# Attention weights, keys and queries turned by VectorE in 32x32 blocks through DRAM instead of by TensorE

## The chip, the cores and the metric

The kernel runs on one core of a Trainium2 chip. The metric is the device time of one execution in microseconds (us). Before the change the median of three runs is 1805.57 us (1801.99 to 1807.5). The engines are named as in the profile: PE is TensorE (PEld its loading of weights), DVE is VectorE, ACT is ScalarE, POOL is GpSimd, SP is SyncE. SP and ACT each have a queue through which they issue DMAs. A difference of less than 0.3% (5.4 us) can't be told from none with runs like these.

## The reference

A backbone of two layers over 256 latent tokens and 256 context tokens of width 2048, in fp32. The even layer has 16 attention heads of width 128 and a state-space mixer side by side, the odd layer a gated short convolution. Only the attention part matters here:

```python
q = rms_norm(heads(cols(p, COL_Q, NA_WIDTH, 0), NA_HEADS, NA_HEAD_DIM), q_norm_g)
k = rms_norm(heads(cols(p, COL_K, NA_WIDTH, 0), NA_HEADS, NA_HEAD_DIM), k_norm_g)
...
s_lat = jnp.einsum('bqhd,bkhd->bhqk', qr, kb) * scale + bias      # per row of the token grid
s_lat = jnp.where(mask, s_lat, -jnp.inf)
s_ctx = jnp.einsum('bqhd,bkhd->bhqk', qr, k_ctx) * scale
pr = jax.nn.softmax(jnp.concatenate([s_lat, s_ctx], axis=-1), axis=-1)
ya = pr[..., :n] @ vb + pr[..., n:] @ v_ctx
ya = ya * jax.nn.silu(gate)
```

So a head has 256 queries and 512 keys. Every product is done with about fp32 precision: each operand is split into a high part and a low rest in the type fp32r, and three products are summed (high x high, low x high, high x low).

## The kernel before

**Work on TensorE.** Nearly all of its time goes into the projections: the weight matrices come in blocks of 128x1024 (512 KB) by SP's queue into five `raw` buffers (L379), ACT casts each into `wH` (L409), DVE subtracts to get `wL` (L416), and PE multiplies (L198). There are three `wH` and three `wL` buffers, so ACT and DVE can prepare two blocks ahead of the one that PE uses. A raw buffer is free for the next load when DVE's subtraction is done.

**Attention.** The heads come in four groups of four, `a` = 0 to 3. When the projections of a group are done, `kq_gen` (L927) takes the products of queries (2 tiles of 128 tokens x 4 heads) and keys (4 tiles): squares summed on ACT (L936), the reciprocal root on POOL, the norm on DVE into a `tmp` tile (L945). To multiply queries by keys, head width has to lie on the partitions; so each tile is turned by four TensorE transposes of 128x128 (`turn`, L202) into a PSUM bank, and ACT (keys, L962) or DVE (queries, with the gains of the norm, L964) copies it to `KT` or `QT`. `head_gen` (L998) then does one head: the splits `kH`, `kL`, `qH`, `qL` (L1041 to L1045), the scores for two tiles of 128 queries, maximum and bias on DVE (L1019), the exponent on ACT (L1024), the division by the sum on DVE (L1028, L1029). The weights have to be turned too: per query tile four TensorE transposes into a bank, then `PH` by ACT (L1065) and `PL` by DVE (L1067), and twelve products with the values, whose result goes through DVE (L1087) and `put_mix` to a DRAM tensor `mixd`. After all heads and the state-space groups, `mix_gen` reads `mixd` back, and the output projection runs in three sweeps over 16 pairs of rows, the last two of which in their order are heads 12 to 15. `res_gen` adds the gated result to x, `turn_gen` turns that for the odd layer.

**What sets the order.** Each engine runs its instructions in the order in which the program issues them. That order is made while the program is built: pieces of work are Python generators that stop at each point where an engine would have to wait, and a planner (`Plan`, L42) holds an estimated time for every engine and every part of a tile. A generator goes on when its operands are due by that estimate (`may`, L247); PE's stream is the projection, into which the other work is put as soon as it is due. `force` (L300) runs generators when the projection itself needs something. Queues of generators are `urgent`, `side` (the heads) and `back` (the matrix-vector products for the modulation). A generator holds a share of ten `tmp` and nine `half` tiles; `("grow", t, h)` waits until it can have so many, `("cap", t, h)` gives back.

**DMA in the planner.** `add` (L96) counts 450 ns of the engine for an issue; a transfer by ACT's queue is done 1500 ns after the bytes at 270 bytes per ns, which start not before what SP's queue still has to move.

## Time and profile before

| what | value |
|---|---|
| median of three runs | 1805.57 us |
| the profiled execution's own time | 1800.62 us |
| its span, first to last instruction | 1798.8 us |
| PE busy | 1765.1 us, 98% |
| PEld busy | 1493.6 us, 83% |
| DVE busy | 1302.0 us, 72% |
| ACT busy | 796.7 us, 44% |
| DMA | 376.92 MB, mean 210 GB/s |
| granted clock of TensorE | 0.999 |

The profiled execution lies 4.95 us below the median of the runs and just below the fastest of them. Busy time of PE is the union of its matmuls, which overlap one another; so a share of 98% tells that PE hardly ever stands idle, and what one matmul costs is read from the distance of starts in the timeline.

### The profile page before, as it was taken

How to read it: one execution, taken by the hardware profiler on the slowest of the kernel's cores; microseconds unless marked ns; L12 is line 12 of the kernel's file. 1: busy time of each engine (PE TensorE's matmuls, PEld its weight loads, DVE VectorE, ACT ScalarE, POOL GpSimd, SP SyncE). 2: the span in 40 equal slices, each digit the busy share in tenths (PEclk: the TensorE clock that was granted, in tenths of full speed). 3: DMA queues.
4: the chain of work that ended last, by engine and by line, in shares of the span. 5: the costliest groups of instructions: out<-in, count | busy, mean ns of one | idle time of the engine just before them, and what ended most of it. 6: DMA issues, size and time to landing. Idle time of an engine off the chain costs nothing.

```text
span 1798.8 us, 26647 instructions
## 1 busy us (share of the span) xinstructions
PE 1765.1 (98%) x10057; PEld 1493.6 (83%) x10057; DVE 1302.0 (72%) x2121; ACT 796.7 (44%) x1410; POOL 31.1 (2%) x28
## 2 busy tenths in 40 slices
PE   6999999999999999999999999999999999999998
PEld 4677888888888879888888898888878888888887
DVE  5566777878686877685875787787657777777665
ACT  5322544436252455242454343654445444444442
POOL 0000100001000000000001000000000000000000
PEclk9999999999999999999999999999999999999999
DMA  9987654566656556655574566878857777877564
GB/s 343 343 289 256 194 168 126 156 205 196 201 171 190 156 184 200 191 157 167 171 218 119 163 190 194 233 218 286 282 182 229 242 247 226 263 224 247 188 210 153
DMA packets 249217, 376.92 MB, mean 210 GB/s; under 512 B 32656, under 2 KB 104048, under 8 KB 249088
## 3 DMA queue, kind: packets, MB, share of 16 engines
q1 hardware_dynamic: 239792, 366.64, 65.5%
q10 hardware_dynamic: 9296, 8.57, 1.4%
q8 instruction: 79, 1.29, 0.3%
q14 instruction: 50, 0.41, 0.1%
HBM read 368.70 MB, written 7.77 MB: 209 GB/s over the span
## 4 chain that ended last, share of the span: by engine, by line
PE 91%; DMA 3%; DVE 3%; issue 1%; ACT 1%; SPq 0%; POOL 0%; POOLq 0%; DVEq 0%; ACTq 0%
PE bank L198 89%; PE bank L202 3%; DMA tmp<-dram_csr 2%; DVE wL L416 1%; DMA raw<-in_ada_w 0%; DMA tmp<-dram_mixd 0%; DVE acc L803 0%; DMA tmp<-in_x 0%; DVE hL L752 0%; SPq L566 0%; DVE tmp L1381 0%; DVE tmp L1200 0%; ACT wH L409 0%; DVE half L1396 0%; DVE tmp L748 0%
## 5 line engine op out<-in xcount | busy, mean ns | idle before, releaser
L409 ACT CAST wH<-raw 128x1024 fp32r<-128x1024 f32 (+1 forms) x440 | 459.1, 1044 | 684.7 <-PE bank L198 585.5
L416 DVE TENSOR_TENSOR wL<-raw,wH 128x1024 fp32r<-128x1024 f32 (+1 forms) x440 | 531.9, 1214 | 227.0 <-ACT wH L409 224.3
L198 PE MATMUL bank<-h,wH 128*128 128x512 f32 x1024 | 358.7, 395 | 2.7 <-ACT h L1664 1.5
L198 PE MATMUL bank<-hH,wH 128*128 128x256 f32 (+1 forms) x1040 | 343.2, 330 | 0.9 <-ACT wH L409 0.9
L198 PE MATMUL bank<-hL,wH 128*128 128x256 f32 (+1 forms) x1040 | 337.2, 324 | 0.0
L198 PE MATMUL bank<-hH,wL 128*128 128x256 f32 (+1 forms) x1024 | 331.7, 324 | 1.1 <-DVE wL L416 1.1
L198 PE MATMUL bank<-h,wL 128*128 128x256 f32 x1024 | 287.2, 280 | 0.1
L198 PE MATMUL bank<-wH,hH 128*128 128x512 f32 x640 | 257.4, 403 | 4.8 <-ACT hH L746 2.6
L198 PE MATMUL bank<-wL,hH 128*128 128x512 f32 x640 | 250.1, 391 | 0.3 <-DVE wL L416 0.3
L198 PE MATMUL bank<-wH,hL 128*128 128x512 f32 x640 | 249.8, 391 | 0.1
L803 DVE SCALAR_TENSOR_TENSOR acc<-raw,csil,acc 128x512 f32<-128x512 f32 x256 | 191.8, 749 | 59.8 <-DMA raw<-in_ada_w 45.4
L198 PEld LDWEIGHTS bank<-h,wH 128*128 128x128 f32 x1024 | 192.2, 188 | 48.4 <-issue 2.6
L198 PEld LDWEIGHTS bank<-hH,wH 128*128 128x128 f32 x1040 | 197.9, 190 | 18.7 <-issue 2.0
L198 PEld LDWEIGHTS bank<-hL,wH 128*128 128x128 f32 x1040 | 198.0, 190 | 15.4
L198 PEld LDWEIGHTS bank<-hH,wL 128*128 128x128 f32 x1024 | 194.8, 190 | 17.5 <-DVE wL L416 2.1
L198 PEld LDWEIGHTS bank<-h,wL 128*128 128x128 f32 x1024 | 193.6, 189 | 0.4 <-DVE wL L416 0.4
L198 PE MATMUL bank<-wH,mix 128*128 128x512 f32 x512 | 162.8, 393 | 0.0
L198 PEld LDWEIGHTS bank<-wH,hH 128*128 128x128 f32 x640 | 120.3, 188 | 35.3 <-issue 6.6
L198 PEld LDWEIGHTS bank<-wH,hL 128*128 128x128 f32 x640 | 120.2, 188 | 25.4 <-DVE hL L752 0.6
L198 PEld LDWEIGHTS bank<-wL,hH 128*128 128x128 f32 x640 | 120.3, 188 | 24.6 <-DVE wL L416 1.1
L198 PEld LDWEIGHTS bank<-wH,mix 128*128 128x128 f32 x512 | 96.2, 188 | 20.7 <-issue 0.9
L198 PE MATMUL bank<-wL,mix 128*128 128x512 f32 x256 | 99.9, 390 | 0.0
(259 smaller groups left out, 1790.1 us busy)
## 6 DMA issues: line engine op xcount, KB each, us to landing
raw<-in_w_in SPq DMA_DIRECT2D x209, 512.0 KB
raw<-in_ada_w SPq DMA_DIRECT2D x163, 512.0 KB
raw<-in_sc_in SPq DMA_DIRECT2D x128, 512.0 KB
raw<-in_w_out SPq DMA_DIRECT2D x64, 512.0 KB
raw<-in_sc_out SPq DMA_DIRECT2D x32, 512.0 KB
tmp<-dram_csr SPq DMA_DIRECT2D x32, 256.0 KB
PT<-in_ada_w SPq DMA_DIRECT2D x14, 512.0 KB
yi<-in_ada_w SPq DMA_DIRECT2D x8, 512.0 KB
```

Source lines behind the costliest of these rows:

```text
L198: E(T.matmul(o, l, r, start=start, stop=stop, skip_group_check=True))
L202: E(T.transpose(o, i, ident if k == 128 else ident[:k, :k]))
L409: E(S.copy(H, v))
L416: E(V.tensor_tensor(out=Lo, in0=v, in1=H.bitcast(F32), op=ALU.subtract))
L803: E(V.scalar_tensor_tensor(out=acc, in0=v[:, j], scalar=csil[:, 2 * k + j:2 * k + j + 1], in1=acc, op0=ALU.mult, op1=ALU.add))
```

## The change

- The TensorE transposes of keys, queries and attention weights are gone, with the PSUM banks and the copies that followed them.
- A normed key or query tile (L945, now with its 32-wide pieces in another order: `mixed`, `plain`) is written by ACT's queue to a DRAM tensor `kqd`, and read back in pairs of tiles by `fetch`: four DMAs, each of which fills 32 partitions with pieces of 128 numbers. This does the part of the turning that goes across groups of 32 partitions; DVE does the rest, a transpose of 32x32 blocks within a 128x512 tile (`blocks`) that writes `KT` or `QT`.
- The attention weights go the same way through `ptd`, one fetch per head, two DVE transposes in place; `PH` and `PL` are then made by one instruction of 128x1024 each, from SBUF.
- There is one buffer for what is fetched, D (the former `PT0`), for heads, keys and queries in turn (`dfree`); `PL` has a tile of its own.
- The division by the sum goes from DVE to ACT (`S.mul`); its factor 0.5 and the gains of the query norm move into instructions that were there before.
- In the planner, a DMA into a tile waits no more for another DMA into the same part of it, and counts as landed when the last is; the DVE transposes are issued 2000 ns after their data are due (`DVE+`); their cost is as a reduction's.
- `res_gen` waits until all heads and groups are done before it takes its four `tmp` tiles and loads its rows.

```diff
--- before.py
+++ after.py
@@ -80,7 +80,7 @@
         if e == "DVE":
             if op == "Memset":
                 return n * 0.26 + 60, 90
-            if op in ("Reciprocal", "TensorReduce"):
+            if op in ("Reciprocal", "TensorReduce", "StreamTranspose"):
                 return n * 1.04 + 70, 90
             if len([a for a in ins if self.size(a) >= n]) >= 2 or op == "ISA" or self.psum(ins):
                 return n * 1.22 + 70, 90
@@ -105,7 +105,7 @@
         for k in ki:
             s = max(s, self.w[k] + 60)
         for k in ko:
-            s = max(s, 0.0 if e == "PE" else self.w[k] + 60, self.r[k] + 60)
+            s = max(s, 0.0 if e == "PE" or op == "DMACopy" else self.w[k] + 60, self.r[k] + 60)
         if op == "DMACopy":
             n = 4
             for _, c in outs[0].ap:
@@ -128,7 +128,7 @@
             self.r[k] = max(self.r[k], free)
             self.last[k[0]] = max(self.last[k[0]], free)
         for k in ko:
-            self.w[k] = done
+            self.w[k] = max(self.w[k], done) if op == "DMACopy" else done
             self.last[k[0]] = max(self.last[k[0]], done)
         return b
 
@@ -202,6 +202,20 @@
         E(T.transpose(o, i, ident if k == 128 else ident[:k, :k]))
 
 
+    mixed = lambda ap: ap.rearrange("p (b k i) -> p k b i", b=4, k=4)
+    plain = lambda ap: ap.rearrange("p (k b i) -> p k b i", b=4, k=4)
+
+    def fetch(dst, src):
+
+        n = src.shape[0] // 32
+        for b in range(4):
+            E(DMA2.dma_start(dst[32 * b:32 * b + 32].rearrange("p t (a x) -> p (t a) x", a=4),
+                             bass.AP(tensor=src.tensor, offset=src.offset + 128 * b, ap=[[512, 32], [32 * 512, n], [1, 128]])))
+
+    def blocks(o, i):
+
+        E(V.transpose(o.rearrange("p k (a j) -> p a k j", a=4), i.rearrange("p (a k j) -> p a k j", a=4, k=4)))
+
     urgent, side, back = [], [], []
     got = set()
     HOR = ((urgent, 4500.0), (side, 2500.0), (back, 1500.0))
@@ -254,8 +268,10 @@
             return grow(task)
         if nb and len(free_b) < nb + (0 if isurg else reserve[0]):
             return False
+        late = eng[-1] == "+"
+        eng = eng.rstrip("+")
         now, t = plan.t["PE"], plan.t["ACT" if eng == "AQ" else eng]
-        rdy = plan.ready(aps)
+        rdy = plan.ready(aps) + (2000 if late else 0)
         if eng == "AQ":
             return t <= now + hor and rdy <= t
         if hor < 2000 and nb and sorted(plan.last[b.tensor.name] for b in free_b)[nb - 1] + 3000 > now:
...
@@ -927,6 +943,13 @@
 
+    kqd = drt([4, 768, 512], "kqd")
+    dfree = [True]
+
+    def d_take(name):
+        dfree[0] = False
+        return st([128, 2, 512], "PT0", name=name)
+
     def kq_gen(key, a, ps, nt, stat, dst, banked):
 
         for t in range(nt):
@@ -938,31 +961,29 @@
             give(free_t, jk)
         yield W_("DVE", stat)
         rstd(stat[:, :4 * nt], stat[:, :4 * nt], 128, EPS, 4 * nt)
-        kns = {}
-
-        def norm(t):
-            kn = kns[t] = tmp()
-            E(V.tensor_tensor(out=four(kn), in0=ps[t].rearrange("p (h d) -> p h d", h=4),
-                              in1=stat[:, 4 * t:4 * t + 4].unsqueeze(2).to_broadcast([128, 4, 128]), op=ALU.mult))
+        src = kqd[a, 512 * (key == "Q"):512 * (key == "Q") + 128 * nt]
+
+        for t in range(nt):
+            yield W_("DVE", stat)
+            kn = tmp()
+            E(V.tensor_tensor(out=mixed(kn), in0=plain(ps[t]),
+                              in1=stat[:, 4 * t:4 * t + 4].unsqueeze(2).unsqueeze(3).to_broadcast([128, 4, 4, 32]), op=ALU.mult))
             if banked:
                 give(free_b, ps[t])
-
-        for t in range(nt):
-            yield W_("DVE", stat)
-            norm(t)
+            yield W_("AQ", kn)
+            E(DMA2.dma_start(src[t * 128:(t + 1) * 128], kn))
+            give(free_t, kn)
+        yield ("cap", 0, 0)
         yield when(lambda: not (attn[0] < 8 * (a if key else 0)))
-        for t in range(nt):
-            yield W_("PE", kns[t], nb=1)
-            pt = bank()
-            for h in range(4):
-                turn(pt[:, h * 128:(h + 1) * 128], kns[t][:, h * 128:(h + 1) * 128])
-            give(free_t, kns[t])
-            yield W_("ACT" if key == "K" else "DVE", pt)
-            if key == "K":
-                E(S.copy(dst[:, :, t * 128:(t + 1) * 128], four(pt)))
-            else:
-                E(V.tensor_scalar(out=dst[:, :, t * 128:(t + 1) * 128], in0=four(pt), scalar1=gqk, scalar2=None, op0=ALU.mult))
-            give(free_b, pt)
+        for t in range(0, nt, 2):
+            yield when(lambda: dfree[0])
+            Dk = d_take(f"kqD_{key}{a}{t}")
+            yield W_("AQ", src[t * 128:(t + 2) * 128])
+            fetch(Dk, src[t * 128:(t + 2) * 128])
+            for k in range(2):
+                yield W_("DVE+", Dk)
+                blocks(dst[:, :, (t + k) * 128:(t + k + 1) * 128], Dk[:, k])
+            dfree[0] = True
         got.add((key, a))
 
     def v_gen(a, ps):
@@ -987,7 +1008,8 @@
         got.add((key, a))
 
-    PH, PL = (st([128, 4, 256], f"PT{k}", F32R, name=f"P{'HL'[k]}") for k in range(2))
+    PH, PL = st([128, 8, 4, 32], "PT1", F32R, name="PH"), st([128, 8, 4, 32], "PL", F32R)
+    ptd = drt([16, 256, 512], "ptd")
     kH, kL, vH, vL = (st([128, 512], n, F32R) for n in ("kH", "kL", "vH", "vL"))
     qH, qL = (st([128, 256], n, F32R) for n in ("qH", "qL"))
     s4s = [st([128, 8], f"s4_{k}") for k in range(4)]
@@ -1021,28 +1043,27 @@
             give(free_b, ps)
             E(V.tensor_scalar(out=s4[:, 2 + qt:3 + qt], in0=s4[:, qt:qt + 1], scalar1=-1.0, scalar2=None, op0=ALU.mult))
             yield W_("ACT", sp, s4)
-            E(S.activation(sp, sp, AF.Exp, bias=s4[:, 2 + qt:3 + qt], scale=1.0, accum_out=s4[:, 4 + qt:5 + qt]))
+            ex = sps[qt] = tmp()
+            E(S.activation(mixed(ex), plain(sp), AF.Exp, bias=s4[:, 2 + qt:3 + qt], scale=1.0, accum_out=s4[:, 4 + qt:5 + qt]))
+            give(free_t, sp)
 
         def scale_(qt):
-            sp = sps[qt]
+            yield W_("DVE", s4[:, 4 + qt:5 + qt])
             E(V.reciprocal(s4[:, 6 + qt:7 + qt], s4[:, 4 + qt:5 + qt]))
-            E(V.tensor_scalar(out=sp, in0=sp, scalar1=s4[:, 6 + qt:7 + qt], scalar2=0.5, op0=ALU.mult, op1=ALU.mult))
-
-        def trans(qt):
-            pt = bank()
-            for kt in range(4):
-                turn(pt[:, kt * 128:(kt + 1) * 128], sps[qt][:, kt * 128:(kt + 1) * 128])
+            yield W_("ACT", s4[:, 6 + qt:7 + qt])
+            E(S.mul(sps[qt], sps[qt], s4[:, 6 + qt:7 + qt]))
+            yield W_("AQ", sps[qt])
+            E(DMA2.dma_start(ptd[hd, qt * 128:(qt + 1) * 128], sps[qt]))
             give(free_t, sps[qt])
-            return pt
 
         yield when(lambda: ("K", a) in got and ("Q", a) in got and (hd == 0 or ("qk", hd - 1) in got))
-        yield ("grow", 2, 0)
+        yield ("grow", 3, 0)
         yield W_("ACT", KT[:, h, :], QT[:, h, :])
         E(S.copy(kH, KT[:, h, :]))
-        E(S.copy(qH, QT[:, h, :]))
+        E(S.mul(qH, QT[:, h, :], gqk))
         yield W_("DVE", kH)
         E(V.tensor_tensor(out=kL, in0=KT[:, h, :], in1=kH.bitcast(F32), op=ALU.subtract))
-        E(V.tensor_tensor(out=qL, in0=QT[:, h, :], in1=qH.bitcast(F32), op=ALU.subtract))
+        E(V.scalar_tensor_tensor(out=qL, in0=QT[:, h, :], scalar=gqk, in1=qH.bitcast(F32), op0=ALU.mult, op1=ALU.subtract))
...
@@ -1052,21 +1073,25 @@
         got.add(("qk", hd))
         yield W_("DVE", p1)
         yield from top(1, p1)
-        yield W_("DVE", sps[0])
-        scale_(0)
-        yield W_("DVE", sps[1])
-        scale_(1)
+        for qt in range(2):
+            yield from scale_(qt)
+        yield ("cap", 0, 0)
+        yield when(lambda: dfree[0] and (hd == 0 or ("d", hd - 1) in got))
+        Dt = d_take(f"D{hd}")
+        got.add(("d", hd))
+        yield W_("AQ", ptd[hd])
+        fetch(Dt, ptd[hd])
+        for qt in range(2):
+            yield W_("DVE+", Dt)
+            turned = Dt[:, qt].rearrange("p (a k j) -> p a k j", a=4, k=4)
+            E(V.transpose(turned, turned))
         yield when(lambda: hd == 0 or ("pv", hd - 1) in got)
-        for qt in range(2):
-            yield W_("PE", sps[qt], nb=1)
-            pt = trans(qt)
-            t = slice(qt * 128, (qt + 1) * 128)
-            yield W_("ACT", pt)
-            E(S.copy(PH[:, :, t], four(pt)))
-            yield W_("DVE", PH[:, :, t])
-            E(V.tensor_tensor(out=PL[:, :, t], in0=four(pt), in1=PH[:, :, t].bitcast(F32), op=ALU.subtract))
-            give(free_b, pt)
-        yield ("cap", 0, 0)
+        flat = lambda ap: ap.rearrange("p a k j -> p (a k j)")
+        yield W_("ACT", Dt)
+        E(S.copy(flat(PH), Dt.rearrange("p t x -> p (t x)")))
+        yield W_("DVE", PH)
+        E(V.tensor_tensor(out=flat(PL), in0=Dt.rearrange("p t x -> p (t x)"), in1=flat(PH).bitcast(F32), op=ALU.subtract))
+        dfree[0] = True
...
@@ -1078,13 +1103,13 @@
         po = bank()
         for kt in range(4):
             ks = slice(kt * 128, (kt + 1) * 128)
...
         got.add(("pv", hd))
         yield W_("DVE", po)
         o = half()
-        E(V.tensor_tensor(out=o, in0=po[:, :256], in1=gt[:, h, :], op=ALU.mult))
+        E(V.scalar_tensor_tensor(out=o, in0=po[:, :256], scalar=0.5, in1=gt[:, h, :], op0=ALU.mult, op1=ALU.mult))
         give(free_b, po)
...
@@ -1538,9 +1563,12 @@
     passed = set()
     at = [0]
 
+    side_left = lambda: [t for t in side if t.gen.__name__ in ("head_gen", "group_gen")]
+
     def res_gen(k, c0, ps):
         cols = slice(c0, c0 + 512)
-        yield when(lambda: n_back[0] >= 3)
+        yield when(lambda: n_back[0] >= 3 and attn[0] == 32 and not side_left())
+        yield ("grow", 4, 0)
         yield W_("SP", mrow[0:1])
         g2 = []
         for t in range(2):
@@ -1685,7 +1713,7 @@
-                    spawn(urgent, res_gen(kcol + k, n, ps), 4)
+                    spawn(urgent, res_gen(kcol + k, n, ps))
```

Where the instructions stand. PE, the turning of query and key tiles of group 0 amid the projection's products (`bank<-hH,wH`; `const` is the identity, `tmp` a normed tile; - is before, + the change):

```order
 L198 MATMUL bank_124<-hL_992,wH_136 128x256
 L198 MATMUL bank_124<-hH_987,wL_139 128x256
-L202 MATMUL bank_130<-const,tmp_109 128x128 x4
-L202 MATMUL bank_129<-const,tmp_110 128x128 x4
-L202 MATMUL bank_130<-const,tmp_112 128x128 x4
 L198 MATMUL bank_123<-hH_1128,wH_137 128x256
 L198 MATMUL bank_123<-hL_1133,wH_137 128x256
```

The three bursts of four transposes go, and the products on both sides of them now follow one another. In the whole program PE has 224 transposes less (24 tiles of keys and queries and 32 of weights, four each), and no other product is added or taken away.

ACT, around heads 6 and 7 (`PH` is the high part of a head's weights, `vH` that of its values, `wH` the projection's next weights). Before:

```order
L409 CAST wH_137<-raw_132 128x1024
L1065 CAST PH<-bank_125 128x4x128
L1065 CAST PH<-bank_126 128x4x128
L1074 CAST vH<-Vt 128x512
L409 CAST wH_138<-raw_134 128x1024
L409 CAST wH_136<-raw_135 128x1024
L921 DMA dram_mixd<-half_121 128x256
```

and in the changed kernel:

```order
L1091 CAST PH<-D_4343 128x1024
L1099 CAST vH<-Vt 128x512
L1054 ACTIVATE tmp_106<-tmp_106,s_3_1698 128x512
L425 CAST wH_138<-raw_133 128x1024
L1056 DMA dram_ptd<-tmp_106 128x512
L1054 ACTIVATE tmp_104<-tmp_104,s_3_1698 128x512
L937 DMA dram_mixd<-half_116 128x256
L1056 DMA dram_ptd<-tmp_104 128x512
L425 CAST wH_136<-raw_134 128x1024
L425 CAST wH_137<-raw_131 128x1024
L212 DMA D_4600<-dram_ptd 32x8x128 x4
L425 CAST wH_138<-raw_135 128x1024
```

ACT's stream now holds the division (L1054), two writes and the four reads of a fetch for each head, between the casts of the projection's weights; whatever a read waits for, the next cast waits behind it.

DVE, the same two heads. Before (`PL` is the low part of the weights; L1029 the division):

```order
L1028 RECIPROCAL s_2_1695<-s_2_1695 128x1
L1029 TENSOR_SCALAR tmp_104<-tmp_104,s_2_1695 128x512
L1028 RECIPROCAL s_2_1695<-s_2_1695 128x1
L1029 TENSOR_SCALAR tmp_111<-tmp_111,s_2_1695 128x512
L1006 TENSOR_TENSOR bias_214<-bias_214,const 128x512
L1044 TENSOR_TENSOR kL<-KT,kH 128x512
L1045 TENSOR_TENSOR qL<-QT,qH 128x256
L1067 TENSOR_TENSOR PL<-bank_128,PH 128x4x128
L416 TENSOR_TENSOR wL_140<-raw_132,wH_137 128x1024
```

and in the changed kernel:

```order
L432 TENSOR_TENSOR wL_139<-raw_134,wH_136 128x1024
L1087 STREAM_TRANSPOSE D_4343<-D_4343 128x512
L1232 SCALAR_TENSOR_TENSOR Cl<-half_120,half_121 128x256
L1041 ISA tmp_111,s_3_1698<-bank_128,bias_214 128x512
L1041 ISA s_3_1698 128x1
L1044 TENSOR_SCALAR s_3_1698<-s_3_1698 128x1
L819 SCALAR_TENSOR_TENSOR acc<-raw_135,csil,acc 128x512
L1087 STREAM_TRANSPOSE D_4343<-D_4343 128x512
L432 TENSOR_TENSOR wL_140<-raw_131,wH_137 128x1024
L1093 TENSOR_TENSOR PL<-D_4343,PH 128x1024
```

The two divisions are gone from DVE and two transposes have come in per head, the first of which waits for the fetch; the subtraction of the projection's next low weights (L432) stands behind it.

More of the change, by code (lines that the diff above doesn't have):

```diff
@@ L317, in force @@
                             continue
-                        when_ = max(plan.t["ACT" if eng == "AQ" else eng], plan.ready(f))
+                        when_ = max(plan.t["ACT" if eng == "AQ" else eng.rstrip("+")], plan.ready(f))
                     if best is None or when_ < best[0]:
@@ L1080, in head_gen @@
             ks = slice(kt * 128, (kt + 1) * 128)
-            mm(po[:, :256], vH[:, ks], PH[:, kt, :], kt == 0, False)
-            mm(po[:, :256], vH[:, ks], PL[:, kt, :], False, False)
-            mm(po[:, :256], vL[:, ks], PH[:, kt, :], False, kt == 3)
+            mm(po[:, :256], vH[:, ks], PH[:, :, kt, :], kt == 0, False)
+            mm(po[:, :256], vH[:, ks], PL[:, :, kt, :], False, False)
+            mm(po[:, :256], vL[:, ks], PH[:, :, kt, :], False, kt == 3)
         got.add(("pv", hd))
```

## The prediction

> **What bounds the kernel now.** I read the page's head first, then busy time by stretches, then what is waited for, then single instructions. (Head of the page: busy time, share of the span, instructions; then shares of the chain that ended last.)
>
> ```profile
> span 1798.8 us, 26647 instructions
> PE 1765.1 (98%) x10057; PEld 1493.6 (83%) x10057; DVE 1302.0 (72%) x2121; ACT 796.7 (44%) x1410; POOL 31.1 (2%) x28
> ...
> PE 91%; DMA 3%; DVE 3%; issue 1%; ACT 1%; SPq 0%; POOL 0%; POOLq 0%; DVEq 0%; ACTq 0%
> ```
>
> PE is busy 98% of the span and makes 91% of the chain. Attention lies in the middle of the program, so I asked for that stretch (columns: us, then busy time of PE, PEld, DVE, ACT, POOL, granted clock, DMA share, GB/s):
>
> ```profile
> 215.00:450.00 235.00, 234.44 (x1433) 204.91 (x1432) 189.92 (x349) 113.46 (x235) 8.87 (x5) 1.00 0.58 168
> ...
> 1100.00:1250.00 150.00, 149.14 (x731) 123.00 (x730) 114.19 (x208) 78.72 (x144) 1.43 (x2) 1.00 0.79 242
> sum 1035.00, PE 1031.68 PEld 886.38 DVE 781.82 ACT 460.22 POOL 23.22; mean PE 206.34 PEld 177.28 DVE 156.36 ACT 92.04 POOL 4.64
> ```
>
> In these 1035 us PE is idle 1035 - 1031.68 = 3.3 us, DVE 253 us, ACT 575 us. What leaves PE's stream here leaves the time, and what comes to DVE and ACT costs only what makes PE wait. With 3.3 us idle, little can be won beside the removed work.
>
> **Removed from PE.** 24 tiles of keys and queries and 16 x 2 of weights, four transposes each: 224. How many there are now, and what they cost (group of transposes with its mean length; then PE's timeline, start and length):
>
> ```profile
> L202 PE MATMUL bank<-const,tmp 128*128 128x128 f32 x324 | 45.9, 273 | 0.2 <-ACT KT L962 0.2
> ```
>
> ```profile
> 275.86 0.39 PE L198 MATMUL bank<-hH,wL 128*128 128x512 f32 x1
> 276.09 1.03 PE L202 MATMUL bank<-const,tmp 128*128 128x128 f32 x8
> 276.88 0.48 PE L198 MATMUL bank<-kH,qH 128*128 128x512 f32 x1
> 277.20 0.39 PE L198 MATMUL bank<-kH,qL 128*128 128x512 f32 x1
> 277.43 0.39 PE L198 MATMUL bank<-kL,qH 128*128 128x512 f32 x1
> ```
>
> One lasts 273 ns, but they overlap, so starts count. From the burst's start at 276.09 to the second product behind it at 277.20 are 1.11 us; one product alone takes 0.23 (277.20 to 277.43). The eight cost 0.88, one 0.110. 224 x 0.110 = 24.6 us. Above it lies busy time shared out, 45.9 / 324 = 0.142, or 31.7 us; 0.110 is taken, since it includes the slower start of the product behind the burst.
>
> [...] The row's distance of starts says 0.110 here, and the sum uses it.
>
> The 192 products with the values now read `PH` and `PL` in runs of 32 numbers instead of 256 in a row. No row shows such a read at this size. Bounds: nothing; or double, and 192 products are three groups like this one,
>
> ```profile
> L198 PE MATMUL bank<-PH,vH 128*128 128x256 f32 x64 | 17.9, 280 | 0.0
> ```
>
> whose busy time of 17.9 would come once more each, 54 us. I take nothing, as they do the same work, and give the other end a rival.
>
> **DVE and ACT** (groups by shape: busy time, mean ns):
>
> ```profile
> L416 DVE TENSOR_TENSOR wL<-raw,wH 128x1024 fp32r<-128x1024 f32 x433 | 527.0, 1222 | 226.3 <-ACT wH L409 223.6
> L409 ACT CAST wH<-raw 128x1024 fp32r<-128x1024 f32 x433 | 454.8, 1051 | 666.9 <-PE bank L198 573.8 <-issue 58.2 <-DMA bias<-dram_rpbs 5.7
> L1067 DVE TENSOR_TENSOR PL<-bank,PH 128x512 fp32r<-128x512 f32 x32 | 21.9, 686 | 6.1 <-ACT PH L1065 5.7
> L1065 ACT CAST PH<-bank 128x512 fp32r<-128x512 f32 x32 | 18.2, 586 | 30.5 <-PE bank L202 29.0 <-DVE half L1087 1.5
> L1029 DVE TENSOR_SCALAR tmp<-tmp,s 128x512 f32<-128x512 f32 x32 | 15.6, 487 | 1.1
> L962 ACT COPY KT<-bank 128x512 f32<-128x512 f32 x16 | 8.9, 589 | 8.7 <-PE bank L202 8.7
> L964 DVE TENSOR_SCALAR QT<-bank,gqk 128x512 f32<-128x512 f32 x8 | 5.8, 747 | 2.2 <-PE bank L202 2.2
> L596 ACT ACTIVATE xs<-xs,rx 128x512 f32<-128x512 f32 x8 | 5.4, 716 | 5.8 <-POOL rx L555 5.8
> ```
>
> DVE loses 15.6 (L1029) and 5.8 (L964); `PL` goes from 21.9 to 16 x 1.222 = 19.6, -2.3. It gains 56 block transposes of 128x512. None is in the trace: between 0.487 (L1029, same shape) and 1.222 (twice the shape); 0.686 is taken, one tensor in and out at L1067's pace: 38.4 us. Net +14.7 us (+3.6 to +44.7) against 253 idle. ACT loses 8.9 (L962), and `PH` goes from 18.2 to 16 x 1.051 = 16.8, -1.4; it gains 32 divisions at 0.716 (L596, same shape and a scale), +22.9. Net +12.6. The query gains, now folded into `qH` and `qL`, the factor 0.5 and the other order of the norm and the exponent's output change forms, not counts: nothing.
>
> **DMAs.** ACT's queue gets 56 writes of 256 KB and 28 fetches of four DMAs, 112. Issue times (ACT's `mixd` write of 128 rows; SP's bias read in 64 x 4 pieces, as many as the 32 x 8 of one fetch DMA: min/median/max ns):
>
> ```profile
> L921 ACTq DMA_DIRECT2D dram_mixd<-half x32: 321/328/623, 285.9 to 1217.5; - x32
> ...
> L1001 SPq DMA_DIRECT2D bias<-dram_rpbs x64: 573/614/1828, 229.1 to 1166.3; - x64
> ```
>
> 56 x 0.328 + 112 x 0.614 = 87 us (168 x 0.328 = 55 to 56 x 0.623 + 112 x 1.828 = 240). With 12.6 that is 100 of ACT's 575 idle us. A fetch holds ACT 4 x 0.614 = 2.5 us. In bytes 56 x 0.262 MB each way is 29.4 MB over the 935 us from 215 to 1150, 31 GB/s; at the rate of the first stretch (0.58 for 168 GB/s) that is 0.11 more DMA share: about 0.69 there, 0.90 in the last. Weights should still come in time.
>
> **New waits.** ACT waits for a write to land before its fetch, with the next `wH` cast behind it; DVE waits for the fetch, with the next `wL` behind it. What such waits did to PE so far (waits: us, times, longest; then a moment on ACT, and that stretch):
>
> ```profile
> ACT wH L409 <- PE bank L198: 599.0, 281, 6.4
> ...
> ACT tmp L1366 <- DMA tmp<-dram_csr: 18.7, 13, 3.0
> ACT mix L1521 <- DMA tmp<-dram_mixd: 10.5, 8, 4.4
> ...
> ACT wH L409 <- DMA bias<-dram_rpbs: 5.7, 1, 5.7
> ```
>
> ```profile
> 957.80 1.05 ACT L409 CAST wH<-raw 128x1024 fp32r<-128x1024 f32 x1 [5.72 <-DMA bias<-dram_rpbs]
> ```
>
> ```profile
> 950.00:960.00 10.00, 10.00 (x57) 8.25 (x57) 5.99 (x13) 3.56 (x13) 0.69 (x1) 1.00 0.72 191
> ```
>
> ACT's casts mostly wait for PE: 599 us in 281 waits, 2.1 each, is its lead. Waits for DMAs took 18.7 + 10.5 + 5.7 = 34.9 us in 22 cases, 1.6 each; the longest, 5.7 us, fell where PE stayed busy 10.00 of 10 us. PE's idle time in the whole stretch, 3.3 us, is a tenth of the 34.9. The change adds 56 waits (28 on ACT, 28 on DVE). If all of them wait 1.6 us and a tenth comes through, that is 9 us; but of the loads with such waits,
>
> ```profile
> tmp<-dram_csr SPq DMA_DIRECT2D x32, 256.0 KB
> ...
> tmp<-dram_mixd ACTq DMA_DIRECT2D x16, 256.0 KB
> ```
>
> 21 of 48 were late, so I take about half, 4 us, between 0 and 9.
>
> A moved stall: `res_gen` loads its rows only when all heads are done. Its sum waited for the end of the first sweep before, too, and sweep two (projection work of PE) covers the load; without that cover it is one load, at most the 4.4 us of the longest `mixd` wait. Counted at nothing.
>
> **Sum.** Against the profiled execution's own 1800.6: 1800.6 - 24.6 + 4 = 1780.0. The median of the runs lies 5.0 above that execution, so 1785 is the forecast for a median. Its own range goes from 1777 (28 us removed, midway between 24.6 and 31.7, and no stall: 1800.6 - 28 + 5) to 1793 (9 us of stalls: 1790, and 3 for the spread of the runs, 1801.99 to 1807.5).
>
> **Rivals.**
>
> *The tail of attention is laid bare.* Heads 12 to 15 come late, since their values are projected last, and the first output sweep needs them. They go through one D buffer in turn. It is held for the fetch's issue 2.5, landing (say the longest `mixd` wait, 4.4), two transposes 1.4, `PH` 1.05, `PL` 1.22: 10.6 us a head. For it: the stretch from 1100 is the fullest on DMA (0.79). Against: 14 of the sweep's 16 pairs of rows need none of them. If two turns are not covered, PE stands 21 us: 1785 - 4 + 21 = 1802, no measurable change.
>
> *Slower: ACT's lead is not enough.* A fetch holds ACT 2.5 + 1.6 = 4.1 us against a lead of 2.1. If the 2.0 over it reach PE each time, 28 x 2.0 = 56 us are lost: 1785 - 4 + 56 = 1837. It is slower from 24.6 / 28 = 0.88 us per fetch on. Against it speaks the stall of 5.7 us that PE did not feel. [...]
>
> *Runs of 32 slow the products with the values.* At double, +54 us by busy time: 1839. Nothing in the profile speaks for it but that no row has such reads.
>
> *More is won*: 31.7 us and no stall, 1800.6 - 31.7 + 5 = 1774. Against: there are 3.3 idle us to win and the starts say 0.110.
>
> That the transposes would stay is excluded: they are not in the changed stream of PE.
>
> **Numbers.** Forecast 0.70, tail 0.13, ACT's lead 0.07, runs of 32 0.03, more 0.07. Time 1785 us. Range 1774 to 1802: it holds the forecast's 1777 to 1793, the better case and most of the tail. With a bound of 0.3% (5.4 us, what such a measurement can tell), faster is below 1800.2: 0.70 + 0.07 + 0.03 of the tail's 0.13 = 0.80; same the rest of the tail, 0.10; slower 0.07 + 0.03 = 0.10.
>
> **What would show it.** Right: 100 transposes of `tmp` left in L202's line; PE's busy time down by about 25 us; PE idle from 215 to 1250 below 10 us; block transposes near 0.69 us; fetch issues near 0.61 us. Wrong: casts of `wH` that wait long for `ptd` or `kqd` with PE idle at those moments (ACT's lead); idle PE amid the first output sweep (tail); a mean well over 280 ns for the products with the values (runs of 32).

## The result, and the profile after

The changed kernel takes 1828.51 us (median of four, 1826.97 to 1834.7) against 1806.24 of the kernel before on the same chip (1801.99 to 1807.5): 1.0134 times as long, with a 95% interval from 1.0105 to 1.0163. It is slower; the forecast was 1785 us, and the range ended at 1802. The profiled execution took 1829.55 us.

The head of its page, then busy time by stretches (columns as in the prediction):

```profile
span 1827.6 us, 26482 instructions
PE 1760.8 (96%) x9833; PEld 1480.6 (81%) x9833; DVE 1309.6 (72%) x2121; ACT 807.9 (44%) x1410; POOL 35.7 (2%) x28
...
PE 58%; DMA 10%; DVE 6%; issue 1%; ACT 1%; SPq 0%; ACTq 0%; POOL 0%; DVEq 0%; POOLq 0%
```

```profile
215.00:450.00 235.00, 220.33 (x1283) 191.86 (x1282) 173.59 (x308) 108.31 (x219) 8.73 (x4) 0.96 0.64 188
...
715.00:980.00 265.00, 256.30 (x1380) 216.74 (x1379) 199.27 (x333) 109.13 (x187) 5.44 (x4) 0.99 0.71 211
...
1100.00:1250.00 150.00, 143.12 (x736) 119.55 (x736) 113.78 (x208) 75.38 (x140) 2.35 (x2) 0.97 0.74 226
sum 1035.00, PE 997.60 PEld 849.60 DVE 775.08 ACT 460.39 POOL 27.81; mean PE 199.52 PEld 169.92 DVE 155.02 ACT 92.08 POOL 5.56
```

PE has 224 instructions less, and yet its busy time fell by 4.3 us only. It stands idle 1827.6 - 1760.8 = 66.8 us in the span, 33.7 before; in the 1035 us around attention 37.4, 3.3 before. And the granted clock, 1.00 in these stretches before, is 0.96, 0.99 and 0.97. Over the whole span it is 0.989 (0.999 before):

```profile
core 0: 1827.6 us, clock 0.989
```

1.1% of 1827.6 is 20.1 us and 0.1% of 1798.8 is 1.8, so some 18 us went to a lower clock. That closes the balance nearly: +33.1 idle, +18.3 clock, -24.6 removed work is +26.8; the spans differ by 28.8.

The parts of the change themselves, in the groups by shape (and, for the fetch, the durations of its issues, min/median/max ns):

```profile
L202 PE MATMUL bank<-const,tmp 128*128 128x128 f32 x100 | 16.0, 285 | 6.5 <-ACT tmp L1128 6.5
...
L1087 DVE STREAM_TRANSPOSE D<-D 128x512 f32<-128x512 f32 x32 | 22.2, 701 | 7.9 <-DMA D<-dram_ptd 7.6 <-issue 0.3
...
L217 DVE STREAM_TRANSPOSE KT<-kqD_K 128x512 f32<-128x512 f32 x16 | 10.4, 686 | 0.0
...
L198 PE MATMUL bank<-PH,vH 128*128 128x256 f32 x64 | 18.2, 285 | 1.1 <-DVE s L1041 0.9 <-ACT vH L1099 0.2
```

```profile
L212 ACTq DMA_DIRECT2D D<-dram_ptd x64: 309/462/767, 288.9 to 1232.6; - x64
```

All of it is about as cheap as estimated: 100 transposes are left, a block transpose takes 0.69 to 0.70 us, the products with the values 285 ns (280 before). The loss is in the waits (us, times, longest):

```profile
ACT wH L425 <- PE bank L198: 482.1, 248, 6.3
...
ACT tmp L1391 <- DMA tmp<-dram_csr: 33.3, 12, 4.5
...
DVE bias L1028 <- DMA bias<-dram_rpbs: 26.6, 11, 5.2
...
ACT wH L425 <- DMA kqD_K<-dram_kqd: 14.6, 2, 9.6
...
DVE tmp L1350 <- DMA tmp<-dram_exr: 11.8, 10, 2.4
...
ACT wH L425 <- DMA D<-dram_ptd: 9.4, 2, 6.3
...
DVE D L1087 <- DMA D<-dram_ptd: 7.6, 2, 5.5
```

ACT's time ahead of PE shrank from 599.0 to 482.1 us. It waits for fetches, and waits that have nothing to do with the new transfers grew too: for `csr` from 18.7 to 33.3, and DVE's for `bias` to 26.6 from this row of the kernel before:

```profile
DVE bias L1006 <- DMA bias<-dram_rpbs: 1.2, 2, 0.9
```

How a wait for a fetch reaches PE, from the timelines of ACT, DVE and PE (start, length; in brackets the idle time before):

```profile
741.00 1.82 ACTq L212 DMA_DIRECT2D kqD_K<-dram_kqd  x4
742.93 2.00 ACT L425 CAST wH<-raw 128x1024 fp32r<-128x1024 f32 x2 [9.64 <-DMA kqD_K<-dram_kqd]
748.72 0.62 ACT L1062 CAST kH<-KT 128x512 fp32r<-128x512 f32 x1 [3.79 <-DVE KT L217]
...
739.66 1.30 DVE L217 STREAM_TRANSPOSE KT<-kqD_K 128x512 f32<-128x512 f32 x2
744.01 1.23 DVE L432 TENSOR_TENSOR wL<-raw,wH 128x1024 fp32r<-128x1024 f32 x1 [3.05 <-ACT wH L425]
747.39 1.30 DVE L217 STREAM_TRANSPOSE KT<-kqD_K 128x512 f32<-128x512 f32 x2
...
749.80 0.49 PE L198 MATMUL bank<-kH,qH 128*128 128x512 f32 x1 [1.97 <-ACT qH L1063]
```

The second fetch of keys could be issued only at 741.00, when DVE had turned the first (739.66 + 1.30 = 740.96): there is one buffer. The cast behind it on ACT had waited 9.64 us, DVE's subtraction 3.05 for that cast, and PE 1.97 for `qH`, which ACT makes behind `kH`, its copy of the turned keys. The stretches before, around and behind this gap, in the view by stretches:

```profile
741.00:746.00 5.00, 5.00 (x24) 4.14 (x23) 1.95 (x3) 2.00 (x2) 0.00 (x0) 1.00 0.41 120
746.00:751.40 5.40, 2.88 (x12) 1.85 (x11) 5.36 (x8) 1.03 (x2) 0.00 (x0) 1.00 0.91 297
751.40:754.80 3.40, 3.40 (x9) 2.65 (x8) 3.29 (x8) 1.77 (x3) 0.00 (x0) 0.50 0.76 219
```

PE is without work for 2.5 us here (5.40 - 2.88, in two gaps), and then it gets half the clock for 3.4 us: nine matmuls are under way in them, against 24 in the 5 us from 741. By these rows, as an estimate, a stall with such a spell behind it costs its own length and then some 1.7 us (half of 3.4) or more.

Other long gaps of PE stand behind an old load, with no fetch in between. Two places, DVE's row ahead of PE's:

```profile
430.07 0.69 DVE L1028 TENSOR_TENSOR bias<-bias,const 128x512 f32<-128x512 f32 x1 [2.89 <-DMA bias<-dram_rpbs]
431.95 0.58 PE L198 MATMUL bank<-hH,wL 128*128 128x256 f32 x1 [4.03 <-DVE wL L432]
...
1202.68 0.69 DVE L1028 TENSOR_TENSOR bias<-bias,const 128x512 f32<-128x512 f32 x1 [4.61 <-DMA bias<-dram_rpbs]
1206.35 0.80 PE L198 MATMUL bank<-kH,qL 128*128 128x512 f32 x1 [3.13 <-DVE qL L1066]
```

DVE waits for `bias`, makes `wL` or `qL` behind it, and PE stands 4.03 and 3.13 us until they are there: 7.2 of the 37.4 us. The gaps at 750 us (1.97 and 0.55) stand behind a fetch. The longest, 6.51 us at 240.56, has two waits of ACT ahead of it, which the view puts down to a fetch (4.52) and to `bias` (3.93). How the rest divides is open.

### The profile page after: what moved, and what is told of

Its sections match the earlier page's. It is cut to its first block, busy times and chain, and to the rows that moved or that the text cites. A ratio compares the mean times of both kernels' runs of the same rounds, so it can differ in the third digit from the quotient of the medians.

```text
span 1827.6 us, 26482 instructions
## 1 busy us (share of the span) xinstructions
PE 1760.8 (96%) x9833; PEld 1480.6 (81%) x9833; DVE 1309.6 (72%) x2121; ACT 807.9 (44%) x1410; POOL 35.7 (2%) x28
## 3 DMA queue, kind: packets, MB, share of 16 engines
q10 hardware_dynamic: 47824, 37.94, 6.6%
## 4 chain that ended last, share of the span: by engine, by line
PE 58%; DMA 10%; DVE 6%; issue 1%; ACT 1%; SPq 0%; ACTq 0%; POOL 0%; DVEq 0%; POOLq 0%
PE bank L198 58%; DMA raw<-in_ada_w 3%; DVE wL L432 2%; DMA bias<-dram_rpbs 1%; DMA raw<-in_w_in 1%; DVE acc L819 1%; DMA tmp<-dram_csr 1%; DMA tmp<-dram_mixd 1%; DMA tmp<-dram_exr 1%; ACT wH L425 1%; PE bank L202 1%; DMA D<-dram_ptd 0%; DMA acc<-in_ada_b 0%; DMA tmp<-in_x 0%; DMA dram_ptd<-tmp 0%
## 5 line engine op out<-in xcount | busy, mean ns | idle before, releaser
L432 DVE TENSOR_TENSOR wL<-raw,wH 128x1024 fp32r<-128x1024 f32 (+1 forms) x440 | 531.3, 1211 | 198.0 <-ACT wH L425 194.9
```

The costliest lines, as they stand in the source:

```text
L432: E(V.tensor_tensor(out=Lo, in0=v, in1=H.bitcast(F32), op=ALU.subtract))
```

## The experiments

Times are medians; ratios are to the kernel before on the same chip, with 95% intervals. "Idle" is PE's over the span (33.7 us before, 66.8 after).

**Is it any other order?** The planner makes the order from estimated times, so the smallest edit to it gives another one. Both kernels with 440 instead of 450 ns for an issue:

```diff
-            self.t[e] = s + 450
+            self.t[e] = s + 440
```

> The kernel before with one constant of the planner moved by nothing that matters: a DMA's issue counts 440 ns instead of 450. No work is added or removed, but the order is made anew in part. Theory draw: the order before is one of few with hardly a stall of PE, and any new order has some; then this is 5 us or more slower than before (1807). Theory late data: only the changed kernel's own round trips make stalls; then this is within 0.3% of before.

> The changed kernel with the same constant moved, 440 for 450. Draw: it differs from the changed kernel's 1828 by 5 us or more, up or down. Late data: within 5 us of 1828, since the same fetches are waited for.

The kernel before: 1808.72 us, 1.0017 [1.0002, 1.0032]. The changed one: 1826.33, 1.0113 [1.0089, 1.0137]. This neutral edit moves either by some 3 us at most, and neither comes near the other. One edit is a small sample of orders, though: another edit to the planner, further down, costs the kernel before 45 us.

**The planner's new DMA rule**, alone in the kernel before; taken back in the changed kernel; kept there for ACT's queue only:

```diff
-            s = max(s, 0.0 if e == "PE" else self.w[k] + 60, self.r[k] + 60)
+            s = max(s, 0.0 if e == "PE" or op == "DMACopy" else self.w[k] + 60, self.r[k] + 60)
...
-            self.w[k] = done
+            self.w[k] = max(self.w[k], done) if op == "DMACopy" else done
```

> The kernel before with nothing but the planner's new rule on DMAs (a DMA waits for no earlier write of its tile, the last landing counts). Three theories stand. Round trip: the new data come late, ACT and DVE wait for them in order, PE runs dry; then this is within 0.3% of before (1806). Planner: the rule makes SP's old loads (bias, exr, the row for acc) look earlier than they are, and DVE is sent to wait for them; then this is 8 us or more slower than before, with long DVE waits for bias. Traffic: the added DMAs delay others by issue, by the 16 engines or by the completion semaphores that the queues share; then this is as before.

> The changed kernel with the planner's old rule on DMAs. Planner: at least half of the loss goes, 1815 or less. Round trip and traffic: it stays within 10 us of 1828; the four DMAs of a fetch are now planned one after the other, so heads come later, but their waits should be shorter.

> The changed kernel with the new rule kept for ACT's queue alone (the fetches), SP's loads planned as before. Planner: 1808 or less, and the DVE waits for bias (26.6 us in 11) fall to a few us. Round trip and traffic: 1820 to 1832.

Alone it costs: 1821.99 us, 1.0082 [1.0058, 1.0106], some 15 us, idle 44.2. The waits of that run:

```profile
ACT tmp L1366 <- DMA tmp<-dram_csr: 34.3, 13, 5.0
...
DVE bias L1006 <- DMA bias<-dram_rpbs: 18.1, 11, 2.6
```

These are the waits that grew in the changed kernel: the rule plans SP's loads into parts of one tile side by side, so their users come earlier, ahead of the landing. A gap of PE of 3.83 us at 700 us stands right behind two waits for `bias` (2.58 and 1.00); the other long one, 5.18 us at 1248, stands at a read of `mixd`. So the rule costs 15 us in the order that it makes; that all of them come from `bias` and `csr` isn't shown. Taken back in the changed kernel, it costs more: 1899.76 us, 1.0509 [1.0479, 1.0539], with one gap of 34.9 us, which no theory had; and with the rule for ACT's queue only it is no faster, 1835.3, 1.0152 [1.0131, 1.0172], above the ranges of all three. DVE's waits for `bias` are gone there, and gaps of 8.6 us before a load of `mixd` and of 5.0 and 3.3 us elsewhere have come in.

**The transfers by themselves.** The kernel before, which still turns its weights on PE, also writes them to `ptd` and fetches them into a tile that nothing reads (32 writes, 64 fetch DMAs; the new rule for ACT's queue only):

```diff
+        for qt in range(2):
+            yield W_("AQ", sps[qt])
+            E(DMA2.dma_start(ptd[hd, qt * 128:(qt + 1) * 128], sps[qt]))
+        yield W_("AQ", ptd[hd])
+        fetch(spareD, ptd[hd])
```

> The kernel before, with the attention weights also written to DRAM and fetched by ACT's queue into a tile that nobody reads (32 writes, 64 DMAs of fetches); PE still turns them, nothing waits for the fetched data but the next fetch. Traffic: 10 us or more slower than before. Round trip: at most 4 us slower, for nobody waits. Planner: at most 4 us slower, since SP's loads are planned as before.

1823.53 us, 1.0086 [1.0064, 1.0107], though no instruction uses the data. Waits of that run:

```profile
ACT tmp L1380 <- DMA tmp<-dram_csr: 16.3, 9, 3.9
...
ACT PH L1079 <- DMA spareD<-dram_ptd: 9.1, 1, 9.1
ACT wH L416 <- DMA spareD<-dram_ptd: 8.7, 2, 4.3
```

ACT still waits for the fetches, which all fill one tile, 17.8 us in three cases. Is this ACT's queue, in which casts stand behind the fetches? The same order with these DMAs issued by POOL's queue (`nc.gpsimd`), counted in the plan as ACT's, and the same in the changed kernel with its whole round trip:

> The kernel before, with the weights' round trip to an unread tile as in the traffic run (32 writes, 64 fetch DMAs), issued by POOL's queue; the order on PE, DVE and SP is the same as in that run, 1823.5 us. Theory A (ACT's queue): nothing waits for these DMAs and ACT has none of them, so 1803 to 1812, as the kernel before. Rival B (bytes and landing of the other loads): 1818 to 1828, since the bytes are the same.

> The changed kernel; its 56 writes to kqd and ptd and 112 fetch DMAs are issued by POOL's queue instead of ACT's. The planner counts them as ACT's, so the order on PE, DVE, SP and ACT is otherwise the same, instruction by instruction. Theory A (what is lost hangs on ACT's queue: the issue of 168 DMAs, each of which can wait for an earlier transfer, with the projection's casts behind it): the gaps of PE that end with ACT go, 240.56 (6.5 us) first, PE's idle time falls from 66.8 to below 50 us, the half-clock time from 37.5 to below 20, and the time to 1795 to 1812. Rival B (it hangs on the transfers themselves: their bytes on the DMA engines and the moment of landing): the same gaps within 10 us of PE idle, 1820 to 1835. Rival C (POOL's own issue is slow and the data come still later): DVE's waits for D and kqD grow and the time goes above 1835.

1825.1 us, 1.0098 [1.0072, 1.0124], and 1842.6, 1.0193 [1.0158, 1.0227]. For the transfers that nothing uses, ACT's queue is not it (theory A falls). The changed kernel came out above 1835 us, and DVE's waits for `D` grew from 7.6 to 29.0 us, which is rival C; so its run doesn't tell what ACT's queue costs there. The two runs with unused transfers agree, 1.0086 by ACT's queue and 1.0098 by POOL's.

Then, is it the transfers, or the order that the planner makes when it counts them? The planner counts the same DMAs, and none is issued; what is left is the same, instruction by instruction:

```diff
-            E(DMA2.dma_start(ptd[hd, qt * 128:(qt + 1) * 128], sps[qt]))
+            E(None, (ptd[hd, qt * 128:(qt + 1) * 128], sps[qt]))
...
```

> The kernel before in the planned order of the traffic run (1823.5 us; by POOL's queue 1825.1), but without that traffic: the planner counts the 32 writes and 64 fetch DMAs, and none is issued. Every engine has the same instructions in the same order as in the traffic run, less these DMAs. Theory T (the transfers' bytes and landings make the loss): 1803 to 1812, as the kernel before, and no half-clock time. Theory O (the order that comes out of the planner makes it: other loads are used closer to their landing): 1817 to 1827, with gaps at the same moments, at 542 us and 1207 to 1252 us.

1810.32 us, 1.0019 [1.0005, 1.0032]. Pages (PE's busy time; ACT's queue: packets, MB, share) and clock of the run without the transfers, then of the one with them:

```profile
PE 1767.8 (98%) x10057; PEld 1493.8 (83%) x10057; DVE 1298.7 (72%) x2121; ACT 798.2 (44%) x1410; POOL 32.7 (2%) x28
...
q10 hardware_dynamic: 9296, 8.57, 1.4%
```

```profile
core 0: 1807.6 us, clock 0.998
```

```profile
PE 1776.3 (98%) x10057; PEld 1498.5 (82%) x10057; DVE 1300.4 (71%) x2121; ACT 798.0 (44%) x1410; POOL 32.6 (2%) x28
...
q10 hardware_dynamic: 31312, 25.36, 4.8%
```

```profile
core 0: 1821.7 us, clock 0.995
```

The order costs some 3 us, the transfers (16.8 MB, 3.4% of the DMA engines' time) some 12 more: 1.0086 - 1.0019 = 0.0067. Of the 14.1 us between the spans, 5.6 are idle time (39.8 and 45.4), and about 5.5 lie in the clock.

Which loads the transfers hold up is seen in part only. The sum of ACT's waits for `csr` is no larger with them than without (16.3 and 21.7 us). SP's queue waits 57.2 instead of 42.6 us for earlier loads of `in_ada_w`. PE's one new gap of 3 us (3.20 at 1207 us) has a wait of ACT for `csr` of 3.08 us ahead of it, 0.45 at that place without the transfers. Nor does the run tell bytes from the number of DMAs: what the completion semaphores, named with the first of these runs, do to the time is not shown. SP's loads, which use nothing of the round trip, were in two cases released by one of its fetches (3.3 us); in the changed kernel SP's loads of weights waited in two cases for a write to `kqd` (5.4 us) and in one for a fetch of queries (3.3 us).

The same question for the changed kernel: every instruction at its place, but small transfers. (Only 32 of 128 rows are written and one of eight pieces per partition fetched, so the turned data are not the right ones. A small fetch reads rows of the first of its two writes only, so it doesn't wait for the second.)

```diff
-            E(DMA2.dma_start(dst[32 * b:32 * b + 32].rearrange("p t (a x) -> p (t a) x", a=4),
-                             bass.AP(tensor=src.tensor, offset=src.offset + 128 * b, ap=[[512, 32], [32 * 512, n], [1, 128]])))
+            E(DMA2.dma_start(dst[32 * b:32 * b + 32, 0, 0:128],
+                             bass.AP(tensor=src.tensor, offset=src.offset + 128 * b, ap=[[512, 32], [1, 128]])),
...
-            E(DMA2.dma_start(src[t * 128:(t + 1) * 128], kn))
+            E(DMA2.dma_start(src[t * 128:t * 128 + 32], kn[:32]), (src[t * 128:(t + 1) * 128], kn))
...
```

> The changed kernel with every instruction at its place, but small transfers: each write to kqd and ptd moves 32 of 128 rows (64 KB instead of 256), each fetch DMA 32 pieces of 512 bytes instead of 256 pieces (16 KB instead of 128), so the turned data are not the right ones; D is cleared once by POOL. The number of DMAs, what waits for them and the planned order are those of the changed kernel; the bytes fall from 29.4 to 5.4 MB. Theory T (the transfers' bytes delay themselves and the other loads): PE idle falls from 66.8 to 45 us or less, half-clock time from 37.5 to 15 or less, 1785 to 1805. Theory W (the waits as such, by the number of DMAs and the fixed part of a landing): 1818 to 1830.

1808.94 us, 1.0005 [0.999, 1.002]. Its queue and waits:

```profile
q10 hardware_dynamic: 17360, 14.09, 2.5%
```

```profile
ACT tmp L1400 <- DMA tmp<-dram_csr: 32.8, 13, 4.0
...
DVE bias L1037 <- DMA bias<-dram_rpbs: 24.1, 11, 4.3
```

Against the changed kernel (q10 there: 47824 packets, 37.94 MB) that is 0.0129, some 23 us: what the size of the transfers costs, be it the bytes or the number of pieces, which this run makes small together. The waits for the second writes are in it too; the changed kernel has one row of ACT waiting for such a write, 3.6 us. The time lies between the two theories, and PE is still idle for 51.0 us (1811.8 - 1760.8). What the run leaves are the waits for `csr` and `bias`, as long as in the changed kernel (32.8 and 24.1 us against 33.3 and 26.6).

**Later landings in the plan.** The planner counts every DMA that touches the program's own DRAM tensors as landed 2000 ns later, in both kernels:

```diff
+            if any(a.tensor.name.startswith("dram") for a in ins + outs):
+                done = done + 2000
```

> The changed kernel; in the planner every DMA that reads or writes a DRAM tensor of the kernel's own (kqd, ptd, csr, exr, bias, mixd) counts as landed 2000 ns later than before. Late data: the work that needs them is put where they are there, the waits for D, bias, csr and exr fall to a few us in sum, and the time falls by 15 us or more, to 1813 or less. Draw: stalls move elsewhere, 1815 to 1840.

> The kernel before with the same 2000 ns in the planner. Late data: within 0.3% of before, or a little faster, as ACT's waits for csr (18.7 us) shrink. Draw: 5 us or more slower than before.

The changed kernel gains: 1815.74 us, 1.0048 [1.0029, 1.0066], less than the theory of late data had. The kernel before loses: 1852.62, 1.0254 [1.0235, 1.0273], by a new order alone. Two others start from the changed one with late landings: the round trip by POOL's queue in the same order, and with it `res_gen`'s eight row loads behind the last read of `mixd`:

```diff
-            yield when(lambda: at[0] >= 9 + 3 * t or k in passed)
+            yield when(lambda: mH[2 * order[15] + 1] is not None or k in passed)
```

> The changed kernel with the planner's landing 2000 ns later (1815.7 us) and, in the same order, the round trip of weights, keys and queries by POOL's queue. Theory A: 1785 to 1805, which would be a version no slower than the kernel before. Rival B: 1812 to 1820.

> The changed kernel with landing counted 2000 ns later and POOL's queue (1808.5 us), and res_gen's eight row loads (2 MB, issued from 1232 us on, just ahead of the last read of mixd) moved behind that read. If these loads delay the last mixd read: the gap of 7.8 us at 1247 and its 10.2 us of half clock shrink to below 4 us together, 1793 to 1800. If that read is late for its own landing alone (write, then read, some 5 to 7 us each): the gap stays, 1805 to 1811.

1808.45 us, 1.0001 [0.9984, 1.0018], between its two theories, and 1807.99, 0.9988 [0.9971, 1.0004]: no difference between the two that can be measured. The gap at the last `mixd` read got smaller, from 7.8 to 5.7 us, and did not go; the moved loads are at most a small part of it. From there, the block transposes planned 4000 instead of 2000 ns after their data, by POOL's queue and, in the same order, by ACT's; then landings 3000 ns later; then the planner's rule for the round trip only:

```diff
-        rdy = plan.ready(aps) + (2000 if late else 0)
+        rdy = plan.ready(aps) + (4000 if late else 0)
```

> As the run with res_gen's loads behind the last read, and DVE's block transposes planned 4000 instead of 2000 ns after their data are due. Theory L (what is left is the landing of the fetches, used too early by the plan): the gaps before KT and D transposes (4.3 us at 247, 4.9 us at 473) go, 8 to 14 us less than that run. Theory O (each new order has its own gaps): within 6 us of it, or slower.

> As the run with the block transposes planned 4000 ns later (1802.6 us), with the round trip on ACT's queue again; the order is the same. The traffic runs on the old kernel gave 1823.5 us with ACT's queue and 1825.1 with POOL's, so if the queue is of no account: 1799 to 1807. If ACT's casts behind the fetches cost something here: 1808 to 1816.

> As the run with res_gen's loads behind the last read, and landing counted 3000 instead of 2000 ns later for all DMAs that touch the program's own DRAM tensors. Theory L: 4 to 12 us less than that run, since bias, csr and the fetches are planned later. Theory O: anywhere from 15 us less to 30 us more, by gaps at new moments.

> As the run with the block transposes planned 4000 ns later (1802.6 us, POOL's queue), and the planner's new DMA rule for the round trip alone, so that SP's loads (bias, csr, exr) are again planned one after the other and used later. Theory S (what is left is mostly SP's loads used too early under the new rule, as in the run of the rule alone, 14.7 us on the old kernel): the gap of 4.0 us at 697 behind bias goes, 1790 to 1800. Theory O (the rule moves so much of the order that the gaps come up elsewhere, as with the rule for ACT's queue alone): 1803 to 1830.

| run | median us | ratio |
|---|---|---|
| 4000 ns, POOL's queue | 1802.6 | 0.9974 [0.9958, 0.9989] |
| 4000 ns, ACT's queue | 1814.18 | 1.0037 [1.0024, 1.0049] |
| landings 3000 ns later | 1812.61 | 1.0022 [1.0001, 1.0044] |
| rule for the round trip only | 1811.04 | 1.0020 [1.0005, 1.0034] |

The first is the only version that beats the kernel before, by 0.11 to 0.42%. It gained 5.4 us on the run that it started from, less than the 8 to 14 of theory L, and it is the best of the twelve versions here that turn the data, so part of it may be a lucky order. Its waits, with one of the same order by ACT's queue behind them:

```profile
DVE bias L1030 <- DMA bias<-dram_rpbs: 11.5, 8, 3.0
...
ACT tmp L1393 <- DMA tmp<-dram_csr: 8.1, 6, 2.2
```

```profile
ACT wH L427 <- DMA D<-dram_ptd: 7.8, 2, 5.5
```

Planned late, the loads are mostly there when they are used (`csr` 8.1 us, 33.3 in the changed kernel), and then the queue does count: by POOL's, no cast stands behind a fetch, and the same order is some 11 us shorter. In the changed kernel's own order POOL's queue brought a loss; there DVE's waits for `D` were 29.0 us (7.6 by ACT's queue):

```profile
DVE D L1087 <- DMA D<-dram_ptd: 29.0, 7, 7.2
```

The last two rows of the table are new orders with new gaps, as theory O had it: 7.3 us at 486 us with 3000 ns, 4.3 at 975 and 3.7 at 1138 with the rule for the round trip only. So what the rule costs can't be read off by taking it back.

## Why the prediction was wrong

- **Removed work, 24.6 us: right as far as shown.** 100 transposes are left. That the time won is really there shows only in the balance of idle time and clock above, which closes to 2 us.
- **DVE, ACT and the products: right.** 0.686 us was taken for a block transpose, 0.686 to 0.701 was measured; the division takes 0.722 us (median of L1054), where 0.716 was taken from L596. The runs of 32 cost next to nothing (285 ns against 280).
- **DMAs: the size was nearly right, the conclusion wrong.** An issue of a fetch takes 0.462 us, not 0.614. DMA share in the first stretch rose by 0.06, not 0.11; in the last it is 0.74, not 0.90. "Weights should still come in time" asked about the wrong loads: the waits that grew most were for the program's small ones, `csr`, `bias` and `exr`, and for the fetches. And in the kernel before, transfers whose data nothing uses, 3.4% of the DMA engines' time, cost 12 us in an unchanged order.
- **New waits, 4 us: the step that failed.** PE's idle time grew by 33 us, not 4. "A tenth comes through" was worked out from waits that the old order had room for, and from chosen ones: the 34.9 us leave out DVE's waits for `in_ada_w`, 45.4 us in the same view. The changed order has waits in a row, of DVE or ACT for `bias` or a fetch, of the other for that one, and of PE for both, as at 741 to 750 us. And the estimate counted the 56 new waits only; the planner's rule, which the working passed over as it moved no instruction's cost, lengthened the waits on loads that were already there: alone 15 us in the old kernel.
- **What a stall costs: left out.** In the changed kernel every gap of 2.49 us or more from 200 us on, and the two at 750 us together, came with a granted clock of 0.50. That is some 18 us beside the 33 us of idle time. It wasn't in the sum, since the kernel before, with 3.3 us idle, shows no such spell in these stretches.
- **`res_gen`, nothing: not contradicted.** In the one version where it was tried, moving its loads further back made no difference that can be measured, though it took 2 us from one gap.
- **The rivals.** "ACT's lead is not enough" named the direction and one mechanism: casts behind fetches, which wait for the buffer (9.64 us at 741). Given 7%, it was the nearest. It is not the whole: by POOL's queue the unused transfers cost the same, and two long gaps stand behind `bias`. The tail shows nothing like its 21 us: from 1100 to 1250 PE is idle 6.9 us, and the longest gap there is one of the two behind `bias`. In this change the turn on TensorE stayed ahead (1.0134); in the best version the round trip is ahead by 0.1 to 0.4%, so the two aren't far from even.

So the balance of the change, in ratios times 1806: -24.6 removed, +23 for the size of the transfers, and the rest, by difference, 24 + 24.6 - 23 = +26 us, in waits that stay when the transfers are small and in the lower clock that comes with them. About 15 of them are what the planner's rule costs in the old kernel. That the same 15 sit in the changed one is argued from its equal waits, not shown; how the rest divides between the one D buffer, ACT's queue and the order is open. A second D buffer wasn't tried.

## What to carry to other kernels

When an engine is busy 98% and its feeders are planned to arrive just in time, look for what a new transfer does to the loads that are already there, not only for who waits for the new data. Price a stall of the matrix engine with the halved clock that can come with it (0.50 for 3.4 us or more at every gap of 2.49 us or more in the changed kernel, from 200 us on). And to tell transfers from the order that comes with them, keep the order and take the transfers out or make them small; where the order may change, gaps move about and hide what an edit costs.

## What was not expected of the hardware

Short gaps came with half the clock: after 2.5 us of idle in 5.4 us (746 to 751.4) there were 3.4 us at a granted clock of 0.50. In this trace 37.5 us in all are at half clock, in seven spells of 3.4, 6.8 or 10.2 us; gaps of 1.75 and 1.64 us (798 and 815 us) were not followed by one. The length of a gap alone doesn't decide, as the same order shows without and with the transfers (the gap, then the clock behind it):

```profile
1240.28 0.50 PE L201 MATMUL bank<-wH,mix 128*128 128x512 f32 x1 [2.86 <-ACT mix L1538]
...
1241.00:1248.00 7.00, 7.00 (x33) 5.79 (x32) 3.35 (x4) 2.59 (x3) 0.00 (x0) 1.00 0.52 174
```

```profile
389.36 0.38 PE L198 MATMUL bank<-PH,vH 128*128 128x256 f32 x1 [1.40 <-ACT vH L1088]
...
390.40:393.80 3.40, 3.02 (x14) 3.02 (x15) 3.40 (x7) 2.17 (x6) 0.00 (x0) 0.50 0.63 168
```

A gap of 2.86 us left the full clock, and one of 1.40 us, with one of 0.87 just behind it, brought half.

Transfers whose data nothing uses cost 12 us in an unchanged order, while the 16 DMA engines were busy 0.64 to 0.77 of the time in the five stretches of attention (0.58 to 0.73 without them); two of the five, with them:

```profile
215.00:450.00 235.00, 232.40 (x1417) 203.69 (x1416) 185.82 (x342) 113.67 (x235) 8.95 (x5) 0.99 0.65 185
...
1100.00:1250.00 150.00, 144.68 (x717) 118.06 (x715) 108.45 (x208) 73.17 (x138) 1.87 (x2) 0.98 0.77 230
```
